# Preparing the next stage's operands: row blocks loaded and split earlier, subtractions moved from VectorE to GpSimd, another chain of scalings at the end

## The chip, the core and the metric

The kernel runs on one core of a Trainium2 chip. The metric is the time of one execution on the device, in microseconds. The core has five engines with an instruction queue each: TensorE (PE), VectorE (DVE), ScalarE (ACT), GpSimd (POOL) and SyncE (SP); in this kernel every transfer between memory and the core's SBUF is issued by SP. An engine takes its instructions in the order in which they stand in its queue and waits at one until its semaphores allow it.

## The reference

Two request groups (a prompt of 1024 rows, a sample of 512 rows, 1024 channels each, float32) go through one layer and a final norm:

```
h = rmsnorm(x, norm_g)
q, f_fw, f_bw, i, z_a, c_B, c_C, c_x, z_b, g_a, g_b = split(h @ w_in)
o_a = bidirectional gated recurrence of q, i, f_fw, f_bw
p_a = (o_a * silu(z_a)) @ w_a
p_b = (c_B * short_conv(c_C * c_x) * silu(z_b)) @ w_b
y = x + (sigmoid(g_a) * p_a + sigmoid(g_b) * p_b) @ w_o
return rmsnorm(y, final_g)
```

## The kernel before

Every large product is done with float32 operands that are split into a high and a low part (`split`: ACT writes the high part, L63, then DVE subtracts it from the source, L64), and three passes: high by high, low by high, high by low. One product of a 128 by 128 block is one matmul of 512 columns.

The program is a row of phases. First the input projections of the prompt, then those of the sample mixed with the recurrence, then the last third of it, which the change touches. It has five stages: the prompt's `w_b` product (`branch_b_prompt`), the sample's `w_b` product (`branch_b_sample`), the prompt's `w_a` product, the sample's `w_a` product (`branch_a_sample`), and the `w_o` product of all 1536 rows (`output`). A sample stage has eight blocks `j` of 24 matmuls each (`plain`, L77). A prompt stage and the output stage take the rows two blocks at a time (`two_blocks`, L819) with seven half products (L825) in place of eight: sums and differences of the two row blocks (`Rows`: S1 to S4, DVE L791 to L796, and their splits) are multiplied with sums and differences of the second operand (`operands`).

The second operand of a prompt or output stage is made before the stage in four steps (`operands`, one per k). A step loads two tiles of 128 by 1024 (`io<-oz_p`, or `io<-in_w_o` for the last stage), splits B11, and makes T1, T3, T2 and T4 by four subtractions, each followed by its split. The subtractions are the helper `minus`, L736, on DVE. They form a chain in place: T3 needs the tile that T1 left, and so on. The steps are handed out while the stage before still multiplies: during the last gate products of the sample (in the loop around `unit`, which evicts each product, `pp`, from one of two PSUM buffers by an ACT instruction, L625), and after the even blocks `j` of a sample stage (`weights_ahead`). The operands B21 and B22 follow later, called as `last`.

The first row blocks of the next stage are loaded and split in `prepared`, which runs when the sample stage has been written out in full. A row block is loaded into one of two buffers (`w_raw`), which also carry the weight blocks of the sample stage. `io` tiles have seven buffers. The order on ACT, DVE, POOL and SP follows from the scheduler's priorities; it is read from the built program.

The output stage ends each row tile when both halves are there: DVE sums the squares, POOL raises to the power -0.5 (`rsqrt`, L81), DVE scales both halves (L958), SP stores them.

Of the kernel before, what the change touches and what calls it, by code (L numbers as in the profile page):

```python
# [2 lines left out]

# [10 lines left out]
AF = mybir.ActivationFunctionType  # L14
ALU = mybir.AluOpType
# [7 lines left out]
TB = 512  # L23
# [20 lines left out]
def trunk_kernel(ctx: ExitStack, tc: tile.TileContext, xs, w, outs, masks_d, ident_d):  # L44
# [334 lines left out]
    with outer:  # L379
# [339 lines left out]
        def operands(O, names, rows):  # L719

            def step(k):
# [12 lines left out]
                def minus(out, x, y, *users):  # L734
                    if any(n in names for n in users):
                        V.tensor_tensor(out, x, y, op=ALU.subtract)  # L736

# [41 lines left out]
        class Rows:  # L779

            def __init__(self, srcs):
                self.raws = [raw_block(x) for x in srcs]
                self.S = None

            def sums(self, second):
# [15 lines left out]

        def prepared(srcs):

            r = Rows(srcs(0))
            r.first()
            r.sums(0)
            r.sums(1)
            return r

# [9 lines left out]
        def two_blocks(O, r, use, last, later):  # L819
# [21 lines left out]
            else:  # L841
                r.sums(1)
            ahead = Rows(later())
            plus(c21, prod(r.s34, 0, "T3"), c12)
# [13 lines left out]

        def weights_ahead(name, steps):

            whl = [block_weights(w[name], j) for j in range(3)]
            yield None
            for j in range(NH):
                if j + 3 < NH:
                    whl.append(block_weights(w[name], j + 3))
                yield j, whl.pop(0)
                if j % 2 == 0 and steps:
                    steps.pop(0)()
# [7 lines left out]

        def branch_prompt(name, O, last, finish_block, pb=None):

# [18 lines left out]

            r = prepared(srcs)
            products(O, last, r, srcs, use)

        def branch_b_prompt(O, last):
            left_of = {}
# [6 lines left out]

            branch_prompt("w_b", O, last, block)  # L910

        def branch_a_prompt(O, last):
            pb = {}
# [8 lines left out]
            left_of = {}  # L922
            branch_prompt("w_a", O, last, block, pb)

# [9 lines left out]

        def output(O, last):
            xt, ss, halves = {}, {}, {}
# [9 lines left out]
            def use(i, m, h, c, more):  # L946
# [4 lines left out]
                A.activation(ps.tile([P, TB], F32, name="junk"), x, AF.Square, scale=D ** -0.5, accum_out=ss[n][:, h:h + 1])  # L951
                halves[n] = halves.get(n, 0) + 1
                if halves[n] == 2:
                    V.tensor_scalar(ss[n][:, 0:1], ss[n][:, 0:1], ss[n][:, 1:2], EPS, op0=ALU.add, op1=ALU.add)
                    r = rsqrt(wk, ss[n][:, 0:1], "y")
                    for h in range(2):
                        x, cols = xt[n][:, h, :], slice(h * TB, (h + 1) * TB)
                        V.scalar_tensor_tensor(x, x, r, fg[:, cols], op0=ALU.mult, op1=ALU.mult)  # L958
                        store(o_tiles[n][:, cols], x)

            r = prepared(srcs)
            products(O, last, r, srcs, use)

# [23 lines left out]
        load(fg, w["final_g"].to_broadcast([P, D]))  # L987
        branch_b_prompt(O, lambda: last_operands(O, take(0, 1), rows))

        rows = lambda k: oz_x[0][k]  # L990
        act = act_parts(cz_x[1], *take(2, 4))
        O, steps = first_operands(take(5, 3, 6, 0, 1), rows)
        blocks = weights_ahead("w_b", steps)
        next(blocks)
        branch_b_sample(blocks, act)
        branch_a_prompt(O, lambda: last_operands(O, take(2, 4), rows))

        rows = lambda k: w["w_o"][k * P:(k + 1) * P, :]
        act = act_parts(oz_x[1], *take(5, 6))
        O, steps = first_operands(take(0, 1, 2, 3, 4), rows)  # L1000
        blocks = weights_ahead("w_a", steps)
        next(blocks)
        branch_a_sample(blocks, act)
        output(O, lambda: last_operands(O, take(5, 6), rows))


# [32 lines left out]
```

## Time and profile before

| | us |
|---|---|
| three runs | 1933.41 (median), 1932.57, 1936.35 |
| the profiled execution's own time | 1938.16 |
| its span, first to last instruction | 1936.4 |
| PE busy | 1911.7 (99%) |
| DVE busy | 1457.9 (75%) |
| ACT busy | 941.7 (49%) |
| POOL busy | 152.8 (8%) |

The shares are averages over the whole program. The change touches only the last 430 us, and there only the places at which one stage hands over to the next are of interest: where PE has no gap, earlier operands buy nothing.

### The profile page before, as it was taken

How to read it: one execution, taken by the hardware profiler on the slowest of the kernel's cores; microseconds unless marked ns; L12 is line 12 of the kernel's file. 1: busy time of each engine (PE TensorE's matmuls, PEld its weight loads, DVE VectorE, ACT ScalarE, POOL GpSimd, SP SyncE). 2: the span in 40 equal slices, each digit the busy share in tenths (PEclk: the TensorE clock that was granted, in tenths of full speed). 3: DMA queues.
4: the chain of work that ended last, by engine and by line, in shares of the span. 5: the costliest groups of instructions: out<-in, count | busy, mean ns of one | idle time of the engine just before them, and what ended most of it. 6: DMA issues, size and time to landing. Idle time of an engine off the chain costs nothing.

```text
span 1936.4 us, 38016 instructions
## 1 busy us (share of the span) xinstructions
PE 1911.7 (99%) x14772; PEld 1612.7 (83%) x14772; DVE 1457.9 (75%) x2423; ACT 941.7 (49%) x1946; POOL 152.8 (8%) x220
## 2 busy tenths in 40 slices
PE   8999999999999999999999999999999999999898
PEld 8988888888888888887888888888888888888786
DVE  7558787878787878786677578777872558898896
ACT  6433434434343444444587567777683333424432
POOL 1000000000000000002122122222220000000000
PEclk8999999999999999999999999999999999999999
DMA  7466666766667676668855555655544966979852
GB/s 214 125 211 231 234 230 234 236 232 231 235 228 238 224 234 237 222 217 319 283 186 196 213 198 181 220 192 187 194 167 168 331 219 196 298 239 308 274 169 76
DMA packets 306436, 427.35 MB, mean 221 GB/s; under 512 B 26192, under 2 KB 178000, under 8 KB 306256
## 3 DMA queue, kind: packets, MB, share of 16 engines
q1 hardware_dynamic: 306256, 424.93, 65.0%
q8 instruction: 116, 1.90, 0.4%
q14 instruction: 64, 0.52, 0.1%
HBM read 254.98 MB, written 169.87 MB: 219 GB/s over the span
## 4 chain that ended last, share of the span: by engine, by line
PE 87%; DMA 5%; DVE 5%; issue 1%; ACT 1%; SPq 0%; POOL 0%; DVEq 0%; POOLq 0%; ACTq 0%
PE pp L308 39%; PE pp L77 21%; PE pw L825 9%; PE pp L201 5%; PE o L537 3%; PE sc L451 3%; PE u L513 2%; PE pp L70 2%; DMA w_raw<-in_w_a 1%; PE u L500 1%; DVE w_l L64 1%; DVE s_l L64 1%; PE sc L485 1%; DMA io<-oz_p 1%; DMA w_l<-wv_d 1%
## 5 line engine op out<-in xcount | busy, mean ns | idle before, releaser
L308 PE MATMUL pp<-s_h,w_h 128*128 128x512 f32 x1120 | 435.9, 389 | 1.2 <-ACT w_h L63 1.2
L308 PE MATMUL pp<-s_l,w_h 128*128 128x512 f32 x1120 | 435.7, 389 | 0.0
L308 PE MATMUL pp<-s_h,w_l 128*128 128x512 f32 x1120 | 435.7, 389 | 0.0
L63 ACT ACTIVATE w_h<-w_raw 128x512 fp32r<-128x512 f32 (+1 forms) x204 | 141.3, 693 | 230.7 <-PE pp L308 151.7
L77 PE MATMUL pp<-s_h,w_h 128*128 128x512 f32 x632 | 250.6, 397 | 2.0 <-ACT K L132 2.0
L308 PEld LDWEIGHTS pp<-s_h,w_h 128*128 128x128 f32 x1120 | 210.2, 188 | 45.4 <-ACT w_h L63 1.9
L308 PEld LDWEIGHTS pp<-s_l,w_h 128*128 128x128 f32 x1120 | 210.2, 188 | 43.6
L308 PEld LDWEIGHTS pp<-s_h,w_l 128*128 128x128 f32 x1120 | 210.2, 188 | 43.6
L77 PE MATMUL pp<-s_h,w_l 128*128 128x512 f32 x632 | 246.4, 390 | 0.0
L77 PE MATMUL pp<-s_l,w_h 128*128 128x512 f32 x632 | 246.2, 390 | 0.0
L313 DVE TENSOR_TENSOR tmp<-pp,tmp 128x512 f32<-128x512 f32 x240 | 165.5, 690 | 106.2 <-PE pp L308 105.0
L63 ACT ACTIVATE w_h<-w_S 128x512 fp32r<-128x512 f32 x160 | 99.4, 628 | 187.9 <-PE pp L308 80.9
L64 DVE TENSOR_TENSOR w_l<-w_raw,w_h 128x512 fp32r<-128x512 f32 (+1 forms) x204 | 155.8, 765 | 37.6 <-ACT w_h L63 37.1
L825 PE MATMUL pw<-s_h,w_h 128*128 128x512 f32 x392 | 153.4, 391 | 2.6 <-ACT w_h L63 2.6
L825 PE MATMUL pw<-s_h,w_l 128*128 128x512 f32 x392 | 153.3, 391 | 2.6 <-DVE w_l L64 2.6
L825 PE MATMUL pw<-s_l,w_h 128*128 128x512 f32 x392 | 153.2, 391 | 0.0
L435 ACT COPY cat<-K 128x512 f32<-128x512 f32 x168 | 111.6, 667 | 65.5 <-DVE K L437 26.9
L77 PEld LDWEIGHTS pp<-s_h,w_h 128*128 128x128 f32 x632 | 118.8, 188 | 25.5 <-ACT K L132 2.4
L77 PEld LDWEIGHTS pp<-s_h,w_l 128*128 128x128 f32 x632 | 118.6, 188 | 25.3
L77 PEld LDWEIGHTS pp<-s_l,w_h 128*128 128x128 f32 x632 | 118.9, 188 | 23.4
L436 ACT COPY cat<-Q 128x512 f32<-128x512 f32 x168 | 112.0, 667 | 29.2 <-DVE Q L438 22.3
L437 DVE TENSOR_TENSOR K<-K,T 128x512 f32<-128x512 f32 x144 | 108.9, 756 | 22.9 <-ACT cat L435 21.0
(187 smaller groups left out, 3301.5 us busy)
## 6 DMA issues: line engine op xcount, KB each, us to landing
w_raw<-in_w_in SPq DMA_DIRECT2D x80, 512.0 KB, 5.3
ws_d<-w_h SPq DMA_DIRECT2D x160, 256.0 KB, 2.5
ws_d<-w_l SPq DMA_DIRECT2D x160, 256.0 KB, 2.5
w_h<-ws_d SPq DMA_DIRECT2D x79, 512.0 KB, 3.7
w_l<-ws_d SPq DMA_DIRECT2D x79, 512.0 KB, 5.3
fkq_d<-sg SPq DMA_DIRECT2D x48, 256.0 KB, 2.3
v_raw<-in_w_in SPq DMA_DIRECT2D x32, 256.0 KB, 3.4
fkq_d<-sk SPq DMA_DIRECT2D x32, 256.0 KB, 2.3
```

Source lines behind the costliest of these rows:

```text
L63: A.activation(hi, src, AF.Copy)
L64: V.tensor_tensor(lo, src, hi.bitcast(F32), op=ALU.subtract)
L77: T.matmul(out, whl[a][:, k, :], rhs(k, b), start=k == 0 and n == 0, stop=k == KT - 1 and n == 2)
L201: T.matmul(pp, B[f"B{k // 4 + 1}{t + 1}"][a][:, k % 4, c * P:(c + 1) * P], parts[k][b], start=k == 0 and m == 0, stop=k == KT - 1 and m == 2)
L308: T.matmul(bank, hl[x][:, k, :], B[b][y][:, k, :], start=k == 0 and i == 0, stop=k == 3 and i == 2)
L313: V.tensor_tensor(out, p, t, op=ALU.add)
L435: A.copy(ap(cat, 0, [[2 * hs, nb], [hs, 2], [1, hs]]), kall)
L436: A.copy(ap(cat, TB, [[2 * hs, nb], [hs, 2], [1, hs]]), qall)
L437: V.tensor_tensor(kall, kall, ap(t, m + 1, [[2, nb], [-m - 1, 2], [0, hs]]), op=ALU.mult)
L451: T.matmul(k.sc[-1][s * Q32:(s + 1) * Q32, li % 4, c, :], kk[:, o:o + Q32], qq[:, t:t + Q32], start=True, stop=True)
L537: T.matmul(p[:, c, :], l, r, start=m == 0, stop=m == len(mms) - 1)
L825: T.matmul(bank, hl[x][:, c:c + P], O[n][y][:, k, :], start=k == 0 and i == 0, stop=k == 3 and i == 2)
```

## The change

Four things change. (1) The four subtractions of each step run on POOL (`G`) in place of DVE: 48 instructions, 16 for each of three stages. (2) Class `Stage` takes the place of `prepared`: the loads and splits of the next stage's first two row blocks are handed out after blocks 4, 5, 6 and 7 of the sample stage; the loads that came with them (`io` tiles for the epilogue) stay behind, in `others`. (3) The operand steps come after blocks 0, 2, 4 and 5, where they came after 0, 2, 4 and 6. (4) For the last two row tiles, the first half is multiplied with `final_g` on POOL ahead of the norm, and scaled by ACT behind it; the second half is scaled by DVE in two pieces of 256 columns with a store each.

```diff
                 def minus(out, x, y, *users):
                     if any(n in names for n in users):
-                        V.tensor_tensor(out, x, y, op=ALU.subtract)
+                        G.tensor_tensor(out, x, y, op=ALU.subtract)
...
             def __init__(self, srcs):
-                self.raws = [raw_block(x) for x in srcs]
+                self.raws, self.rest = [raw_block(x) for x in islice(srcs, 2)], srcs
                 self.S = None
+
+            def others(self):
+
+                for _ in self.rest:
+                    pass
+                return self
...
-        def prepared(srcs):
-
-            r = Rows(srcs(0))
-            r.first()
-            r.sums(0)
-            r.sums(1)
-            return r
+        class Stage:
+
+            def __init__(self, srcs, use):
+                self.srcs, self.use = srcs, use
+                self.ahead = [self.load, lambda: self.r.first(), lambda: self.r.sums(0), lambda: self.r.sums(1)]
+
+            def load(self):
+                self.r = Rows(self.srcs(0))
+
+            def step(self):
+                if self.ahead:
+                    self.ahead.pop(0)()
+
+            def run(self, O, last):
+                while self.ahead:
+                    self.step()
+                products(O, last, self.r.others(), self.srcs, self.use)
...
-        def weights_ahead(name, steps):
+        def weights_ahead(name, steps, stage):
...
                 yield j, whl.pop(0)
-                if j % 2 == 0 and steps:
+                if j > 3:
+                    stage.step()
+                if j in (0, 2, 4, 5) and steps:
                     steps.pop(0)()
...
-                halves[n] = halves.get(n, 0) + 1
-                if halves[n] == 2:
-                    V.tensor_scalar(ss[n][:, 0:1], ss[n][:, 0:1], ss[n][:, 1:2], EPS, op0=ALU.add, op1=ALU.add)
-                    r = rsqrt(wk, ss[n][:, 0:1], "y")
-                    for h in range(2):
-                        x, cols = xt[n][:, h, :], slice(h * TB, (h + 1) * TB)
-                        V.scalar_tensor_tensor(x, x, r, fg[:, cols], op0=ALU.mult, op1=ALU.mult)
-                        store(o_tiles[n][:, cols], x)
...
+                halves.setdefault(n, []).append(h)
+                final = n > 9
+                cols = lambda h: slice(h * TB, (h + 1) * TB)
+                if len(halves[n]) == 1:
+                    if final:
+                        G.tensor_tensor(x, x, fg[:, cols(h)], op=ALU.mult)
+                    return
+                V.tensor_scalar(ss[n][:, 0:1], ss[n][:, 0:1], ss[n][:, 1:2], EPS, op0=ALU.add, op1=ALU.add)
+                r = rsqrt(wk, ss[n][:, 0:1], "y")
+                for h in halves[n]:
+                    x, out = xt[n][:, h, :], o_tiles[n][:, cols(h)]
+                    if final and h == halves[n][0]:
+                        A.activation(x, x, AF.Copy, scale=r)
+                        store(out, x)
+                        continue
+                    for q in range(0, TB, TB // 2 if final else TB):
+                        e = q + (TB // 2 if final else TB)
+                        V.scalar_tensor_tensor(x[:, q:e], x[:, q:e], r, fg[:, cols(h)][:, q:e], op0=ALU.mult, op1=ALU.mult)
+                        if final:
+                            store(out[:, q:e], x[:, q:e])
+                    if not final:
+                        store(out, x)
```

Most later lines of the changed kernel stand one line further down: L63, L64 and L625 of before are L64, L65 and L626 there. Three places in the built order matter.

ACT, in the sample's last gate products, where the third and fourth steps for the `w_b` stage are split. `pp` is a gate product in PSUM, `s2_h` is B11, `s3_h` T1, `s5_h` T3, `s4_h` T2 and `s6_h` T4. Before:

```order
L625 ACTIVATE io_17402<-pp_17377 128x512
L63 ACTIVATE s2_h_17163<-io_17355 128x512
L63 ACTIVATE s3_h_17165<-io_17355 128x512
L63 ACTIVATE s5_h_17169<-io_17355 128x512
L625 ACTIVATE io_17434<-pp_17409 128x512
L63 ACTIVATE s4_h_17167<-io_17357 128x512
L63 ACTIVATE s6_h_17171<-io_17357 128x512
```

And of the change:

```order
L626 ACTIVATE io_17402<-pp_17377 128x512
L64 ACTIVATE s2_h_17163<-io_17355 128x512
L64 ACTIVATE s3_h_17165<-io_17355 128x512
L64 ACTIVATE s5_h_17169<-io_17355 128x512
L64 ACTIVATE s4_h_17167<-io_17357 128x512
L64 ACTIVATE s6_h_17171<-io_17357 128x512
L626 ACTIVATE io_17434<-pp_17409 128x512
```

The eviction of `pp_17409` moved behind the splits of T2 and T4 of the fourth step; all four splits behind B11 now wait for a subtraction on POOL.

SP, in the sample's `w_a` stage: `w_raw<-m_p` is a row block of the output stage, `io<-in_w_o` a tile of an operand step, `m_s<-io` the store of a finished block, `sga_s` and `pb_s` the block's other operands. Before:

```order
L726 DMA io_19535<-in_w_o 128x1024
L726 DMA io_19537<-in_w_o 128x1024
L933 DMA m_s_80<-io_19467 128x512
L929 DMA io_19553<-sga_s_82 128x512
L930 DMA io_19553<-pb_s_78 128x512
L929 DMA io_19584<-sga_s_82 128x512
L933 DMA m_s_80<-io_19504 128x512
L930 DMA io_19584<-pb_s_78 128x512
L726 DMA io_19615<-in_w_o 128x1024
L726 DMA io_19617<-in_w_o 128x1024
```

And of the change:

```order
L765 DMA w_raw_19535<-m_p_79 128x8x128
L951 DMA m_s_80<-io_19467 128x512
L727 DMA io_19539<-in_w_o 128x1024
L765 DMA w_raw_19537<-m_p_79 128x8x128
L727 DMA io_19541<-in_w_o 128x1024
L951 DMA m_s_80<-io_19504 128x512
L947 DMA io_19557<-sga_s_82 128x512
L948 DMA io_19557<-pb_s_78 128x512
L727 DMA io_19592<-in_w_o 128x1024
L727 DMA io_19594<-in_w_o 128x1024
```

The two row blocks' loads moved ahead of, and between, the third step's loads. Before, they stood behind the fourth step's.

DVE, in the same stretch of the change. `w_l<-w_raw` and `w_l<-S` are the low parts of weights and row blocks, `S` the rows' sums, `s0_l` is B11, `s1_l` T1, `s3_l` T3, `s2_l` T2, `s4_l` T4 of the third step, and `io_19504` the fifth block of the sample:

```order
L65 TENSOR_TENSOR w_l_19501<-w_raw_19498,w_h_19500 128x1024
L949 TENSOR_TENSOR io_19504<-pw_19507,io_19504 128x512
L65 TENSOR_TENSOR w_l_19589<-w_raw_19535,w_h_19588 128x1024
L950 TENSOR_TENSOR io_19504<-io_19504 128x512
L65 TENSOR_TENSOR s0_l_19287<-io_19539,s0_h_19286 128x512
L802 TENSOR_TENSOR S_19641<-w_raw_19537 128x512
L798 TENSOR_TENSOR S_19641<-w_raw_19535,w_raw_19537 128x512
L65 TENSOR_TENSOR s1_l_19289<-io_19539,s1_h_19288 128x512
L803 TENSOR_TENSOR S_19641<-S_19641,w_raw_19535 128x512
L799 TENSOR_TENSOR S_19641<-w_raw_19535,S_19641 128x512
L65 TENSOR_TENSOR s3_l_19293<-io_19539,s3_h_19292 128x512
```

The row block's split `w_l_19589` now stands ahead of the instruction that finishes the fifth block, whose store the fourth step's loads follow on SP, and the rows' sums stand between the splits of the third step. Before, all of these stood behind the fourth step's splits.

## Rows read from the trace of the kernel before

**Rows 1.** The page: busy us, share of the span and instructions of each engine

```profile
PE 1911.7 (99%) x14772; PEld 1612.7 (83%) x14772; DVE 1457.9 (75%) x2423; ACT 941.7 (49%) x1946; POOL 152.8 (8%) x220
```

**Rows 2.** PE's waits from 1600 us on: total us, times, longest us

```profile
PE pw L825 <- ACT w_h L63: 2.6, 2, 1.6
PE pw L825 <- DVE w_l L64: 2.6, 3, 1.2
```

**Rows 3.** Timeline of PE around the output stage's start: start us, us, instruction

```profile
1805.41 0.39 PE L77 MATMUL pw<-s_h,w_l 128*128 128x512 f32 x1
...
1812.91 0.50 PE L825 MATMUL pw<-s_h,w_h 128*128 128x512 f32 x1 [1.00 <-ACT w_h L63]
...
1818.16 0.39 PE L825 MATMUL pw<-s_h,w_h 128*128 128x512 f32 x1
...
1839.32 0.50 PE L825 MATMUL pw<-s_h,w_l 128*128 128x512 f32 x1 [0.80 <-DVE w_l L64]
```

**Rows 4.** Windows: stretch, length, then PE, PEld, DVE, ACT, POOL busy, PEclk, DMA, GB/s

```profile
1640.00:1690.00 50.00, 50.00 (x222) 41.44 (x221) 42.84 (x62) 20.54 (x30) 0.00 (x0) 1.00 0.88 284
1762.00:1785.00 23.00, 23.00 (x103) 19.04 (x102) 21.11 (x33) 8.18 (x12) 0.00 (x0) 1.00 0.88 295
1785.00:1806.00 21.00, 20.80 (x92) 16.90 (x90) 18.11 (x28) 8.60 (x13) 0.00 (x0) 1.00 0.96 322
1806.00:1820.00 14.00, 9.86 (x33) 7.03 (x34) 13.91 (x21) 8.04 (x12) 0.00 (x0) 0.88 0.92 305
```

**Rows 5.** Groups of DVE from 1495 us on: busy us, mean ns, idle before

```profile
L736 DVE TENSOR_TENSOR io<-io 128x512 f32<-128x512 f32 x48 | 33.1, 689 | 1.6 <-DMA io<-in_w_o 0.6 <-DMA io<-cz_p 0.5
```

**Rows 6.** Line L425 on POOL: min, median and max ns of one

```profile
L425 POOL TENSOR_TENSOR T<-F x24: 1040/1042/1420, 893.8 to 1428.4; 128x512 f32<-128x512 f32 x24
```

**Rows 7.** Timeline of POOL at 1428 us, in the recurrence

```profile
1428.44 1.42 POOL L425 TENSOR_TENSOR T<-F 128x512 f32<-128x512 f32 x1 [12.47 <-DVE F L134]
1429.94 2.45 POOL L425 TENSOR_TENSOR T<-T 128x256 f32<-128x256 f32 x3
```

**Rows 8.** Timeline of DVE at the same time

```profile
1428.28 0.69 DVE L437 TENSOR_TENSOR K<-K,T 128x512 f32<-128x512 f32 x1
1428.88 1.53 DVE L438 TENSOR_TENSOR Q<-Q,T 128x512 f32<-128x512 f32 x1
```

**Rows 9.** Timeline of DVE at the first operand step

```profile
1507.44 0.69 DVE L64 TENSOR_TENSOR s_l<-io,s_h 128x512 fp32r<-128x512 f32 x1 [4.32 <-ACT s_h L63]
```

**Rows 10.** Timeline of ACT in the sample's last gate products

```profile
1512.49 1.16 ACT L63 ACTIVATE s_h<-io 128x512 fp32r<-128x512 f32 x2 [0.57 <-DVE io L736]
...
1524.88 0.58 ACT L625 ACTIVATE io<-pp 128x512 f32<-128x512 f32 x1
...
1528.73 0.58 ACT L625 ACTIVATE io<-pp 128x512 f32<-128x512 f32 x1
...
1533.88 0.60 ACT L625 ACTIVATE io<-pp 128x512 f32<-128x512 f32 x1 [2.59 <-PE pp L77]
```

**Rows 11.** Timeline of SP's queue in the sample's `w_a` stage

```profile
1784.73 0.90 SPq L726 DMA_DIRECT2D io<-in_w_o  x2
...
1795.63 0.89 SPq L726 DMA_DIRECT2D io<-in_w_o  x2
```

**Rows 12.** DMA issues from 1780 to 1830: KB each, median us to landing

```profile
io<-in_w_o SPq DMA_DIRECT2D x8, 512.0 KB, 6.1
...
w_raw<-m_p SPq DMA_DIRECT2D x4, 512.0 KB, 6.7
```

**Rows 13.** Timeline of DVE at the split of the seventh weight block

```profile
1786.96 1.22 DVE L64 TENSOR_TENSOR w_l<-w_raw,w_h 128x1024 fp32r<-128x1024 f32 x1
```

**Rows 14.** Timelines of DVE and SP's queue in the last 10 us

```profile
1928.08 1.42 DVE L958 SCALAR_TENSOR_TENSOR io<-io,rs_y,fg 128x512 f32<-128x512 f32 x2 [0.73 <-POOL rs_y L81]
...
1931.89 1.41 DVE L958 SCALAR_TENSOR_TENSOR io<-io,rs_y,fg 128x512 f32<-128x512 f32 x2 [0.73 <-POOL rs_y L81]
...
1928.86 4.80 SPq L959 DMA_DIRECT2D out<-io  x4
```

More of the change, by code (lines that the diff above doesn't have):

```diff
@@ L2 @@
 from functools import partial
+from itertools import islice
 import numpy as np
@@ L842, in two_blocks @@
                 r.sums(1)
-            ahead = Rows(later())
+            ahead = Rows(later()).others()
             plus(c21, prod(r.s34, 0, "T3"), c12)
@@ L875, in branch_b_sample, with branch_prompt @@
                 store(pb_x[1][j], s)
-        def branch_prompt(name, O, last, finish_block, pb=None):
+        def branch_prompt(name, finish_block, pb=None):
             s = {}
@@ L896, in use, with branch_b_prompt @@
                 finish_block(m, t, s[m], u)
-            r = prepared(srcs)
-            products(O, last, r, srcs, use)
-        def branch_b_prompt(O, last):
+            return Stage(srcs, use)
+        def branch_b_prompt():
             left_of = {}
@@ L908, in block, with branch_a_prompt @@
                     store(pb_x[0][m], s.rearrange("p a b -> p (a b)"))
-            branch_prompt("w_b", O, last, block)
-        def branch_a_prompt(O, last):
+            return branch_prompt("w_b", block)
+        def branch_a_prompt():
             pb = {}
@@ L922, in branch_a_prompt @@
             left_of = {}
-            branch_prompt("w_a", O, last, block, pb)
+            return branch_prompt("w_a", block, pb)
         def branch_a_sample(blocks, act):
@@ L933, in branch_a_sample, with output @@
                 store(m_x[1][j], s)
-        def output(O, last):
+        def output():
             xt, ss, halves = {}, {}, {}
@@ L951, in use @@
                 A.activation(ps.tile([P, TB], F32, name="junk"), x, AF.Square, scale=D ** -0.5, accum_out=ss[n][:, h:h + 1])
-                halves[n] = halves.get(n, 0) + 1
-                if halves[n] == 2:
-                    V.tensor_scalar(ss[n][:, 0:1], ss[n][:, 0:1], ss[n][:, 1:2], EPS, op0=ALU.add, op1=ALU.add)
-                    r = rsqrt(wk, ss[n][:, 0:1], "y")
-                    for h in range(2):
-                        x, cols = xt[n][:, h, :], slice(h * TB, (h + 1) * TB)
-                        V.scalar_tensor_tensor(x, x, r, fg[:, cols], op0=ALU.mult, op1=ALU.mult)
-                        store(o_tiles[n][:, cols], x)
-            r = prepared(srcs)
-            products(O, last, r, srcs, use)
+                halves.setdefault(n, []).append(h)
[20 more added lines that the diff above has]
+                        store(out, x)
+            return Stage(srcs, use)
         FIRST, LAST = ("B11", "T1", "T2", "T3", "T4"), ("B21", "B22")
@@ L987, in trunk_kernel @@
         load(fg, w["final_g"].to_broadcast([P, D]))
-        branch_b_prompt(O, lambda: last_operands(O, take(0, 1), rows))
+        branch_b_prompt().run(O, lambda: last_operands(O, take(0, 1), rows))
         rows = lambda k: oz_x[0][k]
@@ L992, in trunk_kernel @@
         O, steps = first_operands(take(5, 3, 6, 0, 1), rows)
-        blocks = weights_ahead("w_b", steps)
+        a_prompt = branch_a_prompt()
+        blocks = weights_ahead("w_b", steps, a_prompt)
         next(blocks)
         branch_b_sample(blocks, act)
-        branch_a_prompt(O, lambda: last_operands(O, take(2, 4), rows))
+        a_prompt.run(O, lambda: last_operands(O, take(2, 4), rows))
         rows = lambda k: w["w_o"][k * P:(k + 1) * P, :]
@@ L1000, in trunk_kernel @@
         O, steps = first_operands(take(0, 1, 2, 3, 4), rows)
-        blocks = weights_ahead("w_a", steps)
+        end = output()
+        blocks = weights_ahead("w_a", steps, end)
         next(blocks)
         branch_a_sample(blocks, act)
-        output(O, lambda: last_operands(O, take(5, 6), rows))
+        end.run(O, lambda: last_operands(O, take(5, 6), rows))
 def _masks():
```

## The prediction

> **What bounds the kernel now.** The page comes first: PE is busy for 99% of the span, DVE for 75%, POOL for 8% [rows 1]. An edit on DVE or POOL can pay only where PE waits for operands. So the view of PE's waits from 1600 us is next. It has little: 2.6 us for ACT's high parts and 2.6 us for DVE's low parts [rows 2]. That total leaves out time in which PE issues slowly, so I went to the timeline around the last hand-over. The last product of the `w_a` stage is at 1805.41, the output stage's third half product starts at 1812.91 after a wait, and its successor of high by high passes is at 1818.16; a last wait of 0.80 is at 1839.32 [rows 3]. The windows say what is lost there. At the `w_b` to `w_a` hand-over PE issues 222 matmuls in 50 us, one every 0.225. At that rate 14 us hold 62; the stretch from 1806 to 1820 has 33 [rows 4]. The 29 missing are 6.5 us, part of them because the granted clock there is 0.88 on average [rows 4]: PE is starved and then runs for a while at the lower of its two levels. At the earlier hand-over nothing is missing. So the change has 6.5 + 0.8 = 7.3 us to win at the last hand-over, nothing at the other two, and a part of the tail after the last product.
>
> In the stretch of the loss DVE is the busy engine: 13.91 of 14 us, after 18.11 of 21 and 21.11 of 23; the DMA share is 0.92 to 0.96 [rows 4]. So DVE's backlog decides when the output stage's operands are ready.
>
> **The subtraction on POOL: price of one.** The line that the change moves ran 48 times on DVE, 689 ns each [rows 5]; back to back, DVE starts such instructions 0.60 apart (1428.28 and 1428.88) [rows 8]. POOL does not run a subtraction of float32 tiles in this stretch, but in the recurrence it runs a two-input operation on 128x512: 1.04 us at the least and in the median, 1.42 at the most [rows 6]. The 1.42 one began at 1428.44 [rows 7], beside a DVE operation with two inputs in SBUF that took 1.53 in place of 0.69 [rows 8]. So where the two meet, POOL loses 0.38 and DVE loses 1.53 - 0.60 = 0.93. A moved subtraction then frees 0.60 on DVE and can cost it 0.93. Bounds for one: DVE gains 0.60 (it never meets) or loses 0.33 (it always meets). I take "nearly always" in the stages in which DVE is busy for over 85% of the time, mostly with operations of two inputs.
>
> The Trainium skill has the rule behind it (SBUF — State Buffer, section "Who interferes with whom"): DVE's second input and GpSimd's reads share a port that one holds for its whole instruction, so the other "fully blocks". The trace agrees in kind, 1.53 beside 1.42 [rows 7, 8]. By the rule's whole 1.04 a stage's 16 subtractions would cost DVE 16 x (1.04 - 0.60) = 7.0 us, and 5.3 by the row's 0.93, which would put the sum below 1.7 us later (an estimate).
>
> **Stage one: gate products.** Before, the first step's low part is at 1507.44 [rows 9], ACT's splits follow in pairs of 1.16, and the evictions sit between them: 1524.88 and 1528.73 stand at once behind other ACT work, 1533.88 waits for PE [rows 10]. A unit is 24 matmuls, 24 x 0.2265 = 5.44 us, so units end near 1523.0, 1528.4 and 1533.9. There are two PSUM buffers: the eviction at 1524.88 must be done by 1528.4, and the one at 1528.73 by 1533.9, or PE waits.
>
> After, the four subtractions of a step are a chain on POOL: 4 x 1.04, plus three hand-overs of about 0.08 (an estimate), plus two collisions of 0.38: 5.16. The next step's first subtraction works on a tile whose B11 is split behind T4's split in ACT's queue: T4 0.58 + 0.10, B11 0.56, DVE's low part 0.69 + 0.10. A step is 7.2 us where a unit is 5.44. The first subtraction starts at 1507.44 + 0.69 + 0.1 = 1508.2, the fourth step at 1508.2 + 3 x 7.2 = 1529.8, and T4's subtraction ends at 1535.0. The eviction of `pp_17409` now stands behind T4's split: it is done at 1535.0 + 0.6 + 0.6 + hand-overs = 1536.8, against 1533.9 wanted. **+2.9 us.** Without collisions a step is 6.4, T4 ends at 1531.9 and the eviction is in time: 0. If three of a step's four subtractions meet, four times 0.38 comes on top: +4.4.
>
> **Stage two: `w_b` sample to `w_a` prompt.** DVE has 42.84 us of work in 50 [rows 4]. Take 16 x 0.60 = 9.6 away and add at most 16 x 0.93 = 14.9: 48.1 of 50. It still fits, so 0. Upper bound +3, if half of the 5.3 falls behind the stage's start; lower bound 0, as nothing is lost there.
>
> **Stage three: `w_a` sample to output.** From 1762 to 1820 DVE does 21.11 + 18.11 + 13.91 = 53.1 in 58 us [rows 4]. Minus 9.6 plus 14.9 is 58.4: with collisions the backlog is no shorter. Without, it is 43.5 and the stall could go. But then SP's order decides. Before, the third and fourth steps' loads are issued at 1784.73 and 1795.63 [rows 11], each lands 6.1 later; a row block takes 6.7 [rows 12]. In the change the first row block takes the buffer that the seventh weight block's split frees at 1786.96 + 1.22 = 1788.2 [rows 13]. It lands at 1794.9, and its split by ACT and DVE (1.0 + 1.22) ends near 1797.2. DVE's queue has the fifth block's finish behind that, SP's queue has the block's store, and then the fourth step's loads: near 1798.9, 3.3 later than 1795.63. They land at 1805.0; B11's split, three POOL subtractions and T2's split take about 6.3: 1811.3. With no stall T2 would be wanted two half products and a little after 1805.6, near 1810.2. So 1.1 us is left of 6.5 even without collisions; with them the chain ends as late as today. I take **0**: DVE's backlog sum stands nearer to the collided bound, and the row blocks that come earlier fill the time that their later place left. Bounds: -6.2 (1.1 left of 6.5, and the wait of 0.80 gone) and +5 (the whole 5.3 of collisions, behind the same chain).
>
> **Tail.** Before, the eleventh row tile's two scalings start at 1928.08 and the last one's at 1931.89, 1.42 and 1.41 for a pair, and SP issues the last four stores from 1928.86 in 4.80 [rows 14]. Now one half of each pair goes to ACT, and the other half is two pieces of 256 columns. The multiplication by `final_g` on POOL lies under the second half's product. A piece of 256 is about 0.4 (an estimate, half of 0.69 and a fixed part). The eleventh tile's pair shrinks from 1.42 to 0.8, so the last product's additions start 0.6 earlier, and the last pair also saves 0.6; but six stores in place of four, 4.80 / 4 = 1.2 apart at worst, stand behind. I take **-0.8**, bounds 0 and -1.5.
>
> **Sum.** +2.9 + 0 + 0 - 0.8 = +2.1 us. The profiled execution, whose own time is 1938.16, would take 1940.3; it lies 4.75 above the median of the runs shown, and I carry the difference over: 1933.4 + 2.1 = 1935.5. The likeliest case's own range is 1931 to 1938.5 (gate term 0 to +4.4, tail 0 to -1.5, last hand-over within 1.5 of today).
>
> **Rivals.** Faster: the subtractions seldom meet a two-input operation, so stage one costs 0 and the last stall shrinks to 1.1. That gives -6.2 - 0.8 = -7.0; with part of the gate term (up to +2.9) it is -7 to -4, about 1927.5. For it: half of all POOL operations in the recurrence took 1.04, not 1.42 [rows 6], and their DVE neighbours are two-input operations too. Against it: at that place POOL is busy 8% of the time, here it would be busy while DVE is at 18.11 of 21 [rows 4]. It decides where fewer than about one in three subtractions meets. Chance 0.25.
>
> Slower: the queues in order. The fourth step's loads stand on SP behind the fifth block's store, which waits for DVE, which stands behind the row block's split. If they are issued after 1798.9, each us goes straight into the stall: DVE's 0.93 for each of the four or so collisions ahead of the store makes it 3.7 later, the stall 10.2 in place of 6.5: 1935.5 + 3.7 = 1939.2. It decides from an issue later than 1799. For it: DVE's share in that stretch; against it: DVE has 2.9 us idle of 21 there. Chance 0.33.
>
> That the change does nothing that can be told (POOL's price hidden, the stall bound by DMA at 0.92 to 0.96 busy [rows 4]) would give the tail alone, 1932.6. It is part of the likeliest case's range; together they have 0.42.
>
> **How the numbers follow.** A measurement of this kernel tells about 0.2% from no change, 3.9 us: 1929.5 to 1937.3 is the same. The first case (0.42) lies in it but for its upper end; I leave 0.34 there, 0.02 below it and 0.06 above. The faster rival is below 1929.5 but for 0.02; the slower rival is above 1937.3 but for 0.04. Faster 0.25, same 0.40, slower 0.35. Range: 1926 to 1942, from the faster rival's -7 to the slower's upper end (+2.1 + 3.7 + 2.7 of the other bounds).
>
> **What would show it.** Stage one is right if ACT's eviction behind T4's split ends near 1536.8 and PE has a gap before its next-but-one unit; wrong if PE issues every 0.2265 to 1566. The price is right if POOL's subtractions take 1.4 and DVE's neighbours about 1.5, wrong at 1.04 and 0.69. Stage three is right if the fourth step's loads are issued near 1798.9 on the old clock and the stretch after 1805.4 again lacks some 29 matmuls; the faster rival shows as fewer than 10 lacking, the slower one as more than 40. The tail is right if the span ends 0.8 less after the last matmul. The prediction is wrong above all if DVE and POOL share time better than the one collided pair in [rows 7, 8] tells.

## The result, and the profile after

The changed kernel takes 1956.89 us in the median of four runs (1955.29 to 1959.60), against 1933.74 before: a ratio of 1.0114, with a 95% interval of 1.0101 to 1.0126. (Ratios in this document are the ones on record, with their intervals; they can differ a little from the quotient of the two medians, here 1.0120.) The forecast was 1935.5 in a range of 1926 to 1942, so it is wrong by 21 us. The profiled execution took 1956.11; its span is 1954.1.

The page's busy line of the changed kernel (answers to [rows 1]):

```profile
PE 1919.9 (98%) x14772; PEld 1616.0 (83%) x14772; DVE 1457.6 (75%) x2375; ACT 941.5 (48%) x1948; POOL 228.7 (12%) x270
```

DVE has 48 instructions fewer and is busy as long as before: 1457.6 us against 1457.9. The 33.1 us that the subtractions took [rows 5] came back somewhere else.

PE's waits from 1490 us on (total us, times, longest us), where before there were two groups of 2.6 us each [rows 2]:

```profile
PE pw L842 <- ACT s_h L64: 5.3, 3, 3.3
PE pp L78 <- ACT io L626: 5.1, 3, 2.1
PE pw L842 <- DVE s_l L65: 4.0, 3, 2.3
PE pw L842 <- DVE w_l L65: 3.0, 4, 1.3
```

They stand at three places, not at one. The windows of the changed kernel around each of them, and one full window for comparison (columns as in [rows 4]):

```profile
1518.00:1542.00 24.00, 18.91 (x74) 14.49 (x73) 15.14 (x14) 9.49 (x17) 14.44 (x10) 0.93 0.70 251
1694.00:1718.00 24.00, 19.79 (x71) 14.73 (x70) 17.14 (x25) 10.55 (x16) 0.35 (x1) 0.86 0.77 265
1600.00:1624.00 24.00, 24.00 (x108) 19.87 (x107) 17.77 (x26) 6.23 (x7) 0.00 (x0) 1.00 0.48 154
1818.00:1862.00 44.00, 35.92 (x139) 27.34 (x138) 38.57 (x55) 19.16 (x34) 9.72 (x7) 0.92 0.72 249
1600.00:1644.00 44.00, 44.00 (x196) 36.44 (x195) 33.88 (x47) 16.30 (x21) 2.71 (x2) 1.00 0.61 198
```

And of the kernel before, the window that answers to the fourth, and a full one:

```profile
1804.00:1848.00 44.00, 38.85 (x159) 30.36 (x159) 39.90 (x61) 18.89 (x32) 1.80 (x2) 0.96 0.78 254
1600.00:1644.00 44.00, 44.00 (x195) 36.44 (x195) 35.01 (x51) 15.35 (x21) 0.00 (x0) 1.00 0.61 200
```

At 0.2265 us for a matmul, the 34 that are missing in the first window are 7.7 us, the 37 in the second 8.4, the 57 in the third 12.9, of which before lost 36 matmuls or 8.2. That is 7.7 + 8.4 + 4.7 = 20.8 us more. Each loss contains a stretch at the lower of PE's two clock levels, which follows the gap: the mean granted clock is 0.93, 0.86 and 0.92. The tail takes some back. The last matmul of before and of the change:

```profile
1927.89 0.39 PE L825 MATMUL pw<-s_h,w_l 128*128 128x512 f32 x1
```

```profile
1946.34 0.39 PE L842 MATMUL pw<-s_h,w_l 128*128 128x512 f32 x1
```

From there to the span's end are 1936.4 - 1927.9 = 8.5 us before and 1954.1 - 1946.3 = 7.8 after. Together that is 20.8 - 0.7 = 20.1 us; the interval of the ratio is 19.5 to 24.4. The two profiled spans differ by 17.7 us only: compared matmul by matmul, the profiled execution of the change was 2.3 us ahead of that of before when it came to the first of these places.

**The price of one subtraction.** The line of the subtractions on POOL (min, median and max ns), and the first two steps of the first stage on POOL:

```profile
L737 POOL TENSOR_TENSOR io<-io x48: 1272/1606/2199, 1506.7 to 1829.9; 128x512 f32<-128x512 f32 x48
```

```profile
1506.75 6.06 POOL L737 TENSOR_TENSOR io<-io 128x512 f32<-128x512 f32 x4 [17.61 <-DVE s_l L65]
1514.87 6.04 POOL L737 TENSOR_TENSOR io<-io 128x512 f32<-128x512 f32 x4 [2.07 <-DMA w_l<-ws_d]
```

DVE beside the first of them:

```profile
1505.92 0.69 DVE L65 TENSOR_TENSOR s_l<-io,s_h 128x512 fp32r<-128x512 f32 x1 [4.98 <-ACT s_h L64]
1508.73 1.22 DVE L65 TENSOR_TENSOR s_l<-io,s_h 128x512 fp32r<-128x512 f32 x1 [2.12 <-ACT s_h L64]
1510.10 1.55 DVE L65 TENSOR_TENSOR s_l<-io,s_h 128x512 fp32r<-128x512 f32 x1
```

A subtraction takes 1.27 us at the least, and 1.61 in the median; the 1.04 of [rows 6] does not occur. DVE's low parts, 0.69 when POOL is idle, take 1.22 and 1.55 beside it. Their group in the kernel before and in the change, from 1495 us on (busy us, mean ns):

```profile
L64 DVE TENSOR_TENSOR s_l<-io,s_h 128x512 fp32r<-128x512 f32 x84 | 56.2, 688 | 13.9 <-ACT s_h L63 13.5
```

```profile
L65 DVE TENSOR_TENSOR s_l<-io,s_h 128x512 fp32r<-128x512 f32 x84 | 77.3, 941 | 37.5 <-ACT s_h L64 35.0
```

21.1 of the 33.1 us come back in this one group. A step is 1514.87 - 1506.75 = 8.12 us long, where a unit of PE is 5.44. The evictions stand behind such steps on ACT, and PE waits for them:

```profile
1522.63 0.50 PE L78 MATMUL pp<-s_h,w_h 128*128 128x512 f32 x1 [2.06 <-ACT io L626]
...
1530.23 0.50 PE L78 MATMUL pp<-s_h,w_h 128*128 128x512 f32 x1 [1.86 <-ACT io L626]
...
1538.72 0.50 PE L78 MATMUL pp<-s_h,w_h 128*128 128x512 f32 x1 [1.17 <-ACT io L626]
```

**The second place** shows how a slow chain passes through four queues. The timelines of POOL, DVE, SP's queue, ACT and PE, in this order, and windows of PE, PEld, DVE, ACT and POOL in the 50 us before that:

```profile
1687.39 6.96 POOL L737 TENSOR_TENSOR io<-io 128x512 f32<-128x512 f32 x4 [3.27 <-DVE s_l L65]
```

```profile
1690.29 2.92 DVE L65 TENSOR_TENSOR s_l<-io,s_h 128x512 fp32r<-128x512 f32 x2 [1.84 <-ACT s_h L64]
1693.36 2.39 DVE L65 TENSOR_TENSOR s_l<-io,s_h 128x512 fp32r<-128x512 f32 x2 [0.15 <-ACT s_h L64]
1695.66 0.68 DVE L893 TENSOR_TENSOR io<-pw,io 128x512 f32<-128x512 f32 x1
```

```profile
1696.37 0.32 SPq L894 DMA_DIRECT2D pb_s<-io  x1
...
1698.66 0.32 SPq L727 DMA_DIRECT2D io<-oz_p  x1
```

```profile
1704.05 0.63 ACT L64 ACTIVATE s_h<-io 128x512 fp32r<-128x512 f32 x1 [7.56 <-DMA io<-oz_p]
```

```profile
1706.15 0.77 PE L842 MATMUL pw<-s_h,w_h 128*128 128x512 f32 x1 [3.34 <-ACT s_h L64]
```

```profile
1640.00:1660.00 20.00, 20.00 (x90) 16.57 (x89) 17.53 (x21) 8.87 (x13) 6.18 (x4) 1.00 0.66 217
1660.00:1680.00 20.00, 20.00 (x90) 16.57 (x89) 15.16 (x17) 7.39 (x11) 7.85 (x6) 1.00 0.87 283
1680.00:1690.00 10.00, 10.00 (x46) 8.29 (x45) 6.40 (x7) 3.75 (x6) 6.49 (x5) 1.00 0.66 220
```

The fourth step's subtractions end at 1694.35, the low parts behind them at 1695.75. A block of the sample is finished only then on DVE (1695.66), though PE had done the last of the sample's products by 1691.4. The block's store on SP follows (1696.37), and behind it, when the store has landed, the load of B21's tile (1698.66), then its split (1704.05) and PE (1706.15). None of these engines is full: in 1680 to 1690 DVE is busy 6.40 of 10 us, ACT 3.75 and POOL 6.49. Each instruction stands behind one that waits.

**The third place** has the loads on time and the loss behind them. SP's queue, DVE, POOL and PE:

```profile
1812.96 0.93 SPq L727 DMA_DIRECT2D io<-in_w_o  x2
```

```profile
1816.32 1.77 DVE L803 TENSOR_TENSOR S<-S,w_raw 128x512 f32<-128x512 f32 x1
```

```profile
1824.62 6.90 POOL L737 TENSOR_TENSOR io<-io 128x512 f32<-128x512 f32 x4 [5.38 <-DVE s_l L65]
```

```profile
1830.56 0.49 PE L842 MATMUL pw<-s_h,w_h 128*128 128x512 f32 x1 [1.59 <-ACT s_h L64]
```

The first line is the fourth step's loads. The rows' sums stand on DVE ahead of that step's B11 and meet the third step's subtractions on POOL (1.77 us in place of 0.69). POOL waits 5.38 us for B11's low part, and PE then waits for the splits behind the chain.

### The profile page after: what moved, and what is told of

The parts are those of the page before. It is cut to its first block, busy times and chain, and to the rows that moved or that the text cites. A ratio compares the mean times of both kernels' runs of the same rounds, so it can differ in the third digit from the quotient of the medians.

```text
span 1954.1 us, 38068 instructions
## 1 busy us (share of the span) xinstructions
PE 1919.9 (98%) x14772; PEld 1616.0 (83%) x14772; DVE 1457.6 (75%) x2375; ACT 941.5 (48%) x1948; POOL 228.7 (12%) x270
## 4 chain that ended last, share of the span: by engine, by line
PE 83%; DMA 5%; DVE 5%; POOL 3%; issue 3%; ACT 1%; SPq 1%; POOLq 0%; DVEq 0%; ACTq 0%
PE pp L309 39%; PE pp L78 19%; PE pw L842 8%; PE pp L202 5%; PE o L538 3%; PE sc L452 3%; POOL io L737 2%; PE pp L71 2%; PE u L514 2%; PE u L501 1%; DVE w_l L65 1%; DMA w_raw<-in_w_a 1%; DMA io<-oz_p 1%; DVE s_l L65 1%; PE sc L486 1%
## 5 line engine op out<-in xcount | busy, mean ns | idle before, releaser
L64 ACT ACTIVATE w_h<-w_raw 128x512 fp32r<-128x512 f32 (+1 forms) x204 | 141.2, 692 | 232.6 <-PE pp L309 153.0
L64 ACT ACTIVATE w_h<-w_S 128x512 fp32r<-128x512 f32 x160 | 99.0, 628 | 190.6 <-PE pp L309 85.1
L65 DVE TENSOR_TENSOR w_l<-w_raw,w_h 128x512 fp32r<-128x512 f32 (+1 forms) x204 | 156.9, 770 | 41.4 <-ACT w_h L64 41.2
L426 POOL TENSOR_TENSOR T<-F 128x512 f32<-128x512 f32 x24 | 28.8, 1201 | 1005.7 <-DMA F<-fkq_d 848.4
```

Of the source, the lines that this page charges most:

```text
L64: A.activation(hi, src, AF.Copy)
L65: V.tensor_tensor(lo, src, hi.bitcast(F32), op=ALU.subtract)
```

## The experiments

The theories on record are A, the subtractions on POOL are a long chain in which the queues of ACT and DVE stand; B, the row blocks that were moved ahead cause the later losses; C, POOL and DVE shut each other out, and so lengthen each other's instructions. Medians are of the run itself and of the kernel before on the same chip.

**The change with the subtractions on DVE** (`e1_sub_dve`):

```diff
-                        G.tensor_tensor(out, x, y, op=ALU.subtract)
+                        V.tensor_tensor(out, x, y, op=ALU.subtract)
```

> The changed kernel with its subtractions back on VectorE; the earlier row blocks, the shifted step and the last chain stay. Theory A (the subtractions on GpSimd are a slow chain in which ScalarE's and VectorE's queues stand): the three places of lost time, 7.5, 9.0 and 4 us more than before, all go, 1925 to 1935 us. Rival B (the loads and splits of row blocks, moved ahead in the queues, cause the loss at the second and third hand-over): 13 us stay, about 1946 us.

1933.09 against 1935.03 us: 0.9988 (0.9979 to 0.9997). B falls as the cause of the loss: without the subtractions on POOL the rest of the change is 2 us faster than before.

**The kernel before with only the subtractions on POOL** (`e2_sub_pool`, the same line in the other direction):

> The kernel before with only its 48 subtractions moved to GpSimd. Theory A: all three places lose, about +20 us, 1950 to 1957. Rival B: only the first place loses, +7.5, about 1941. My prediction's price (a subtraction alone 1.04 us, the second hand-over untouched): about 1937.

1954.93 us, 1.0103 (1.0090 to 1.0117), +20 us: this part is nearly all of the change's +22 (1.0114). Moving the subtractions also moved ACT's evictions behind splits that they had stood ahead of; no run has the one without the other, so what the new order adds by itself is not shown.

**Only the new tail** (`e3_tail`, part 4 of the diff on the kernel before):

> The kernel before with only the new chain of scalings for the last two row tiles. The prediction's step: -0.8 us, about 1933. Rival: six stores in place of four behind each other take it back, 1934 or more.

1934.93 us, 0.9998 (0.9989 to 1.0007). A timing cannot show 0.8 us here. In the profile the last matmul is at 1922.72 and the span ends at 1930.4: 7.7 us, against 8.5. Over all profiles of this document it is 8.5 to 8.8 in the nine with the old tail and 7.7 to 8.0 in the six with the new one. The tail does what was forecast.

**POOL beside, with nobody waiting for it** (`e4_pool_beside`; `fg` is loaded earlier):

```diff
                         V.tensor_tensor(out, x, y, op=ALU.subtract)
+                        G.tensor_tensor(spare, out, fg[:, 0:TB], op=ALU.subtract if "T4" in users else ALU.mult)
```

> The kernel before, all subtractions on VectorE, with one more GpSimd instruction of 128 by 512 behind each of the 48, whose result nobody reads (36 subtractions, 12 multiplications). The engines share as in the change, but nothing waits for GpSimd. Theory A (latency of the chain): within 3 us of before. Rival C (VectorE slowed by sharing with GpSimd): 16 x 0.9 us more of VectorE work in each stage, 5 us or more slower. The price of one where VectorE is idle: 1.28 us for a subtraction if the operation matters and 1.04 for a multiplication; 1.04 for both if only contention lengthened it.

1966.97 us, 1.0166 (1.0152 to 1.0180), +32 us, more than the change itself. DVE keeps its subtractions here, so it carries more than in the change (busy 1501.7 us against 1457.6), and the size is not that of the change; but no engine waits for these instructions, so A cannot explain it. The first instruction on POOL and the one beside it on DVE:

```profile
1507.28 1.30 POOL L737 TENSOR_TENSOR spare<-io,fg 128x512 f32<-128x512 f32 x1 [17.25 <-DMA w_h<-ws_d]
```

```profile
1507.33 1.80 DVE L736 TENSOR_TENSOR io<-io 128x512 f32<-128x512 f32 x1 [0.18 <-DMA io<-cz_p]
```

DVE starts 0.05 us later and ends at 1509.13, which is 0.55 after POOL's end at 1508.58: it stood until POOL had finished. The Trainium skill (SBUF — State Buffer, "Who interferes with whom") says that a DVE instruction with two SBUF inputs contends with a GpSimd instruction that reads SBUF, and that the shared ports are an exclusive lock. The trace agrees: the 0.55 us after POOL's end are nearly a whole instruction of DVE's (0.69).

**The subtraction left out, a memset in its place** (`e5_memset_pool`), and **three memsets** (`e9_memset_three`):

```diff
-                        V.tensor_tensor(out, x, y, op=ALU.subtract)
+                        G.memset(out, 0.0)
```

> The kernel before with each of the 48 subtractions replaced by a GpSimd memset of the same 128 by 512 tile: the subtraction is left out, so the T operands are wrong, but every instruction still waits for GpSimd as in the change, and GpSimd reads nothing in SBUF. Theory A (the latency of the chain on GpSimd): most of the 20 us stays, 1945 or more, unless a memset is far shorter than 1.28 us. Rival C (GpSimd's reads and VectorE's two-input instructions shut each other out): VectorE's splits go back to 0.69 us each, and the time is that of before or a few us less, 1927 to 1937.

> As the run with a memset for each subtraction (which is left out), but three memsets one after another: by the single one's 0.53 us some 1.45 us of GpSimd for each, longer than a subtraction alone (1.28) and still without a read of SBUF. Theory A (the length of the chain on GpSimd): the first place loses as in the change, 7 us, and the later ones some 5: 1940 to 1950. Rival C (shutting out): at most 2 or 3 us above the run with single memsets, 1932 to 1937.

1932.80 against 1934.81 us, 0.9990 (0.9981 to 0.9999); with three memsets 1934.53 against 1935.14, 0.9998 (0.9989 to 1.0007). The low parts of the run with three, and its memsets:

```profile
L64 DVE TENSOR_TENSOR s_l<-io,s_h 128x512 fp32r<-128x512 f32 x84 | 55.2, 687 | 37.7 <-ACT s_h L63 37.7
```

```profile
L737 POOL MEMSET io<- 128x512 f32 x144 | 71.0, 528 | 245.0 <-DMA io<-in_w_o 106.1 <-DMA io<-oz_p 101.7 <-DMA io<-cz_p 17.0
```

POOL is as busy as in the change, and DVE's 687 ns are untouched: the memsets, which only write, did not lengthen the low parts. But DVE has also lost the work of the subtractions.

**Three memsets, and DVE's work kept** (`e11_memset_and_dve`):

```diff
+                        for _ in range(3):
+                            G.memset(out, 0.0)
+                        V.tensor_tensor(spare, out, fg[:, 0:TB], op=ALU.subtract)
```

> As the run with three memsets for each subtraction (which is left out), and VectorE keeps as much work as before: behind each it does one subtraction of 128 by 512 that nobody reads. So GpSimd's chain is as long as in the change and VectorE's load is that of before, and only the shutting out is gone (a memset reads nothing in SBUF). Theory A (length of the chain while VectorE is loaded): 1945 or more. Rival C (shutting out lengthens both engines' instructions, and that is what is lost): 1933 to 1939.

1937.76 against 1935.33 us, 1.0011 (1.0002 to 1.0020). The page's busy lines of the run with the subtractions on POOL and of this one:

```profile
PE 1917.4 (98%) x14772; PEld 1614.6 (83%) x14772; DVE 1458.9 (75%) x2375; ACT 942.7 (48%) x1946; POOL 224.9 (12%) x268
```

```profile
PE 1912.7 (99%) x14772; PEld 1614.8 (83%) x14772; DVE 1455.7 (75%) x2423; ACT 939.9 (49%) x1946; POOL 223.8 (12%) x364
```

The same load on DVE and POOL, and 2.4 us are lost in place of 20. One thing else differs, though. POOL of this run in the first stage:

```profile
1505.64 17.85 POOL L737 MEMSET io<- 128x512 f32 x36 [15.31 <-DMA io<-cz_p]
```

Three steps run without a pause, where the change has 2.07 between two steps. With memsets the scheduler puts the next step's B11 split earlier on ACT, so a hand-over of the chain is gone as well, and these runs do not tell A from C cleanly.

**The shutting out taken from the low parts alone** (`e13_psum_low`, on the kernel of `e2_sub_pool`; `nought` is a tile of zeros in PSUM):

```diff
-                        split(*(z[:, k, :] for z in O[n]), src)
+                            A.activation(hi, src, AF.Copy)
+                            V.tensor_tensor(lo, src, nought, op=ALU.subtract)
```

> The kernel before with its subtractions on GpSimd, and the low parts of the same five operands taken as source minus a tile of zeros in PSUM, not minus the high part in SBUF (so the low parts are wrong). ScalarE's and GpSimd's orders are those of the run with the subtractions on GpSimd, and every wait between the engines stays but the low part's on its high part; VectorE's low parts now have one input in SBUF. Theory A (length of the chain, with the hand-over of 2.07 us between two steps): a step shrinks from 8.1 us only by what GpSimd's instructions get shorter, to 7.4 where 5.44 are wanted, and most of the 20 us stays: 1945 or more. Rival C (shutting out): low parts back at 0.69, subtractions at 1.28, and more than half of the 20 us goes: 1944 or less.

1945.33 against 1934.99 us: 1.0053 (1.0036 to 1.0070). Its first steps on POOL, its subtractions and its low parts:

```profile
1506.77 5.41 POOL L741 TENSOR_TENSOR io<-io 128x512 f32<-128x512 f32 x4 [16.32 <-DVE s_l L737]
1513.63 5.41 POOL L741 TENSOR_TENSOR io<-io 128x512 f32<-128x512 f32 x4 [1.45 <-DMA w_l<-ws_d]
```

```profile
L741 POOL TENSOR_TENSOR io<-io 128x512 f32<-128x512 f32 x48 | 64.1, 1335 | 260.6 <-DVE s_l L737 136.1 <-DMA s_l<-cz_s 103.7 <-DMA io<-in_w_o 9.1
```

```profile
L737 DVE TENSOR_TENSOR s_l<-io,junk 128x512 fp32r<-128x512 f32 x60 | 40.7, 686 | 40.8 <-POOL io L741 35.1 <-DMA io<-cz_p 3.6 <-DMA io<-in_w_o 1.8
```

With one input in PSUM the low parts are back at 686 ns, the subtractions at 1335 on average, and a step at 6.86 us. PE's wait for the evictions in the first stage falls from 4.8 us (three waits, in the run with the subtractions on POOL) to 1.4 (one). The result lies between the two expectations: the loss is 10.3 us in place of 20. But the edit took two things away, the shutting out and the low part's wait for ACT's high part. ACT and DVE, for T4 of the first step and B11 of the second:

```profile
1512.21 1.16 ACT L736 ACTIVATE s_h<-io 128x512 fp32r<-128x512 f32 x2 [0.74 <-POOL io L741]
```

```profile
1512.21 1.28 DVE L737 TENSOR_TENSOR s_l<-io,junk 128x512 fp32r<-128x512 f32 x2 [0.69 <-POOL io L741]
```

Both start at once, where DVE stood behind ACT in the change. Of the 1.26 us by which a step is shorter, 0.65 are the four subtractions (6.06 to 5.41), which is C, and some 0.6 the hand-over (2.07 to 1.45), which is the missing wait. So C is shown to lengthen the step, and about half of the loss goes with C and this wait together; how that half divides between them is not shown. The other half is not split either: a step of 6.86 us is still longer than 5.44, which is A, and the rows' sums, the weights' low parts and part of the blocks' finishes still have two inputs in SBUF, which is C.

**T4's subtraction alone on POOL** (`e6_t4_pool`):

```diff
-                        V.tensor_tensor(out, x, y, op=ALU.subtract)
+                        (G if users == ("T4",) else V).tensor_tensor(out, x, y, op=ALU.subtract)
```

> The kernel before with only T4's subtraction, the last of each step's chain, on GpSimd: 12 instructions. Nothing of the step waits for it but its own split. Theory A (chain): within 1 us of before, since the chain of three stays on VectorE. Rival C (shutting out): each costs VectorE about 1.2 us and frees 0.60, 4 in a stage, +2.4 us of VectorE work in each, 0 to 3 us slower and all of it at the last hand-over.

1937.58 against 1934.81 us, 1.0012 (1.0003 to 1.0021): slower by 2.3 us for the one subtraction behind which nothing of its own step stands but its split. That is on C's side, but the interval begins at 0.6 us, so A's "within 1 us" is not excluded. The profile shows no loss at the first two places (108 matmuls in 24 us at both) and at the third as many as the profile of before (160 in 44 us, against 159).

**What one instruction costs on POOL when DVE is idle** (`e8_price`):

```diff
+                    for op in (ALU.subtract, ALU.mult):
+                        for x, y in ((fg[:, 0:TB], fg[:, TB:D]), (ap(fg, 0, [[2, TB]]), ap(fg, 1, [[2, TB]]))):
+                            for _ in range(2):
+                                G.tensor_tensor(spare, x, y, op=op)
```

> The kernel before with nine more GpSimd instructions of 128 by 512 after the first stage's fourth step, where VectorE is idle; nobody reads them. Two tiles read in full rows, subtract and multiply; every second element, subtract and multiply; two of each. If the operation or the stride sets the price: 1.04 us for the strided multiplications as in the recurrence, 1.28 for the rest. If only the neighbour on VectorE made the difference: all 1.04.

Four of them, in order: a subtraction of full rows, one of every second element, and the two multiplications:

```profile
1533.82 1.29 POOL L755 TENSOR_TENSOR spare<-fg 128x512 f32<-128x512 f32 x1
...
1535.19 1.04 POOL L755 TENSOR_TENSOR spare<-fg 128x512 f32<-128x512 f32 x1
...
1537.43 1.28 POOL L755 TENSOR_TENSOR spare<-fg 128x512 f32<-128x512 f32 x1
...
1540.15 1.04 POOL L755 TENSOR_TENSOR spare<-fg 128x512 f32<-128x512 f32 x1
```

Between these the operation does not matter; the access does. The instruction of [rows 6] reads two interleaved streams of one tile.

**The part that pays.** In three more runs the subtractions are on DVE. `e7_last_only` prepares row blocks earlier for the output stage alone, `e10_sums_first` hands out the sums one place earlier there, and `e12_no_shift` takes the shifted step back:

```diff
-                if j > 3:
+                if j > 3 and name == "w_a":
                     stage.step()
-                if j in (0, 2, 4, 5) and steps:
+                if j in (0, 2, 4, 5 if name == "w_a" else 6) and steps:
```

```diff
-                    stage.step()
+                    for _ in range(2 if j == 5 else 1):
+                        stage.step()
```

```diff
-                if j in (0, 2, 4, 5 if name == "w_a" else 6) and steps:
+                if j % 2 == 0 and steps:
```

> The changed kernel with its subtractions on VectorE, and the earlier row blocks and the shifted step for the output stage alone; the prompt's w_a stage is prepared as in the kernel before. In the run with subtractions on VectorE the hand-over near 1700 us lost 2.6 us that the kernel before did not lose. If the earlier row blocks cause it: another 2 to 3 us faster, about 1930. If it came from something else: the same as that run, about 1933.

> The run with earlier row blocks for the output stage alone, with one more change: there the first sums of the rows and their split are handed out before the fourth operand step, not behind it. In that run TensorE waited 2.5 us for the low part of these sums, which stood behind the fourth step's splits on VectorE. If that place is what ends last: 2 us faster, about 1930.5. If the fourth step's T2 comes late in its place: no change, 1932.4.

> The run with earlier row blocks for the output stage alone, without the shifted step: the fourth operand step is handed out after block 6 again. If the shifted step is what the last hand-over gains from: 2 to 3 us slower than that run, 1935. If the earlier row blocks alone bring it: no change, 1932 to 1933.

1932.38 against 1934.81 us, 0.9985 (0.9976 to 0.9994); 1933.43 against 1935.14, 0.9991 (0.9982 to 1.0000); 1934.90 against 1935.33, 1.0000 (0.9991 to 1.0009). PE's waits from 1490 us on in the first of them:

```profile
PE pw L842 <- DVE w_l L65: 3.3, 3, 2.5
PE pw L842 <- ACT w_h L64: 0.4, 1, 0.4
```

The waits for ACT that [rows 2] has are nearly gone, those for DVE have grown. `e7_last_only` beats both kernels, by 2.9 us over before. The 2 to 3 us that it should have gained over `e1_sub_dve` cannot be told from none in the times (0.9985 and 0.9988). In the profiles they can be seen: from 1688 to 1712 PE does 96 matmuls in `e1_sub_dve` and 107 in `e7_last_only`, 2.5 us, so the row blocks and the step moved ahead for the `w_a` stage do cost something there (one profile each). Handing out the sums earlier brought nothing more. Without the shifted step the gain is not there, but the intervals overlap.

## Why the prediction was wrong

The forecast was +2.1 us and the profiles show +20.1. Stage one accounts for 4.8 of the 18.0 between them, stage two for 8.4 and stage three for 4.7. So the steps that failed are the size of the first term and the two hand-overs that were put at nothing.

**The price of a subtraction** is the step that failed first. It took the nearest row of POOL by shape, 1.04 us and 1.42 beside DVE; measured are 1.28 alone and 1.61 in the median. A row by access was not to be had: the trace of before has no POOL instruction of 128 by 512 that reads two operands in full rows. The collided price on DVE, 0.93, was too high on average: DVE's busy total stayed the same, so the 33.1 us saved were lost again, 33.1 / 48 = 0.69 for each.

**Stage one** was right in its mechanism and too small: a step of 7.2 us was forecast and 8.12 measured, +2.9 and 7.7. The POOL part is 6.06 in place of 5.16, and the hand-over to the next step 2.07, close to the forecast's 7.2 - 5.16 = 2.04. With 1.28 in place of 1.04 the forecast's own sum gives a step of 8.2 and +6.7 (an estimate), so by this estimate the price makes most of the miss. The forecast looked only at the eviction behind the last step; PE waited three times, and its clock fell to the lower level in between.

**Stage two**, taken as 0 with an upper bound of 3, lost 8.4, the largest miss. The term was worked out from DVE's total of work (48.1 of 50). DVE was busy for less than that, 17.53 + 15.16 + 6.40 = 39.1 us in 1640 to 1690 where before had 42.84, and yet PE lost: the total does not decide. Work that fits on average still comes late where each low part waits in its queue for POOL, and a block, a store and a load wait behind it. The forecast followed such a chain for the third stage alone.

**Stage three**, taken as 0 with a bound of 5, lost 4.7, inside its bounds. The fourth step's loads were issued as forecast: 1812.96 is 1799.4 on the clock of before (the change is 13.6 us behind there), against 1798.9. The term failed behind them: from landing to T2's split 6.3 us were taken, which gave 1811.3, but PE got T2's high part only at 1830.56, or 1817.0 on the clock of before, since B11's low part stood behind the rows' sums on DVE.

**The tail** was right, -0.7 to -0.8 in the profiles.

**The rivals.** The slower one named the in-order queues, and these it was, but it looked for late loads at one place and for 3.7 us; the loads came on time, and the time was lost behind them and at two other places. The faster one needed fewer than one in three subtractions to meet a two-input instruction; a median of 1.61 us, where one alone takes 1.28, says that at least half did. What the change gives without the subtractions, 2 us, stayed far below the 7.3 that PE lost at the last hand-over.

## What to carry to other kernels

In these runs an instruction moved from DVE to POOL freed DVE where DVE's neighbours had one input in SBUF, or where POOL's instruction read nothing there; else both lengthened, and DVE's saving came back to the last microsecond (1457.9 us busy before, 1457.6 after). When a step of a chain moves to a slower engine, compare the chain's period with that of the engine that is fed (8.1 and 5.4 us here), and follow what stands behind each waiting instruction in every queue at every hand-over; totals of busy time do not show it. A price should be taken from a row with the same access pattern, not only the same shape. How the 20 us divide between the longer chain and the shutting out is open.

## What the runs showed of the hardware

On POOL, two operands of 128 by 512 float32 that are read in full rows took 1.28 us, and every second element of one tile 1.04, for subtraction and multiplication alike; a memset took 0.53. A DVE instruction with two inputs in SBUF that met a running POOL subtraction or multiplication stood for all of its rest (1.80 us in place of 0.69), while one input in PSUM (686 ns) or a POOL instruction that only writes (687 ns) cost DVE nothing.
